# Feed-forward of a hybrid decoder block: the product of gate and up is turned by VectorE and DMAs in place of TensorE

## The chip, the cores and the metric

The kernel runs on one NeuronCore of one Trainium2 chip. That core has TensorE (PE in the profile; PEld is its weight load), VectorE (DVE), ScalarE (ACT), GpSimd (POOL), and SyncE (SP), whose queue starts nearly all transfers here. The metric is the device time of one launch in microseconds, lower is better.

## The reference

One decoder layer over 512 tokens of 1024 features, all in float32. A token mixer (retention and forgetting attention, merged by gates) comes first; it is left alone here but for its last step. What matters is the end:

```python
x = x + merged @ w_out[l]

h2 = rmsnorm(x, g_ffn[l])
ff = (jax.nn.silu(h2 @ w_gate[l]) * (h2 @ w_up[l])) @ w_down[l]
x = x + ff
```

`w_gate` and `w_up` are 1024 x 2816, `w_down` is 2816 x 1024. The norm's factor per token, `rsqrt(mean(x*x) + eps)`, is applied behind the products, as a scale for each token.

## The kernel before

Activations of the residual stream are held with features on the partitions: `x1[p, m, t]` is feature 128 m + p of token t. A float32 product is made of three matmuls: both operands are split into a rounded high part (made by ScalarE, a cast) and a remainder (made by VectorE, a subtraction), and high by high, low by high and high by low are summed in PSUM.

**Gate and up.** The columns of both weights are cut into six groups, `GROUPS = [512] * 5 + [256]`. Each group's pair of products is computed with a Strassen-like scheme of seven block products (`gu`), in the order y (A12), x (A11), S1, S2, S3, S4, A22. Each is 24 matmuls with a 128 x 128 block of the activations as weights and 512 (in the last group 256) weight columns as the moving side. Activations are stationary, so results have tokens on the partitions: four tiles of 128 tokens each. The blocks' sums (`sum_of`, line 947), their casts (line 938) and remainders (line 939) go through a ring of three buffers (`ring_parts`), and each half of a block feeds 12 matmuls.

Three pairs of accumulators are used: `x_`, `z_` (tag `acc`) and `y_` (tag `sc`). `x_` is started by A11, copied to `us` slot 0 by ScalarE (`keep(0, x_)`, line 1033), and then added to by S2, copied again (slot 1), added to by S3, copied (slot 2), and added to by A22. So S2's first matmul writes a bank that `keep(0)` reads. `z_` is copied once (slot 3).

`us[tp]` is a tile of 4 slots of 512 columns for each of the two token pairs. At a group's end slot 0 and slot 2 hold silu(gate) * up for the four token tiles (lines 1087 and 1094); `hs[g]` names these four views. The tiles have the tags `us0` and `us1` in a pool with one buffer for a tag, so the tile of the next group lies in the same memory.

**Turning.** The down product needs the hidden features on the partitions. `put_h(g, cs)` does it in the next group: for each chunk of 128 hidden features, four TensorE transposes (`turn`, line 75) into a `tp` bank, then one ScalarE copy (line 1023) to `pf[:, chunk, :]`. Two chunks go behind the product y, two in the middle of the product x. The last group's two chunks are turned among the first matmuls of the down product.

**The norm.** In group 0 alone, four small matmuls sum the squares, `rsqrt` (12 tiny VectorE instructions) makes `rstd2`, and then the first gate is scaled (lines 1065 and 1066). In the text this lies ahead of the sums for S3.

**Down.** `whole(k, ms)` adds hidden chunk k (8 to 21) to all 8 output banks; `prepare(k)` loads and splits its operands. `p_sums` and the last loop do chunks 0 to 7 with another Strassen-like scheme. There, `raw` (a weight load) and `u2` use the memory of `us0` and `us1`.

**Order.** TensorE's instructions are pinned in the order in which they are written (`pinned`), and VectorE's in the gate and up stage as well (`queue`). ScalarE's and SyncE's order is set by the tile framework's scheduler when the kernel is built. Semaphores, and the wait of a new tile for the old tile in its memory, are the framework's too.

Of the kernel before, what the change touches and what calls it, by code (L numbers as in the profile page):

```python
# [9 lines left out]
F32 = mybir.dt.float32  # L10
F32R = mybir.dt.float32r
# [3 lines left out]
ALU = mybir.AluOpType  # L15
AX = mybir.AxisListType

P = 128
# [35 lines left out]
def block_kernel(ctx: ExitStack, tc, x, xT, c_early, c_tab, c_late, w_qf, w_tok, w_vg, w_a, w_y, w_o, w_gu, w_gl, w_dn, w_dh, out):  # L54
# [19 lines left out]
    def turn(o, src):  # L74
        in_order(nc.tensor.transpose(out=o, in_=src, identity=ident))  # L75

    def f32(ap):
        return ap.bitcast(F32)
# [12 lines left out]
    def bank(tag):  # L91
        return ps.tile([P, 512], F32, name=tag, tag=tag, bufs={"acc": 4, "sc": 2, "tp": 2}[tag])
# [71 lines left out]
    def gffn(k):  # L164
        return ce[:, C_GFFN + k:C_GFFN + k + 1]
# [229 lines left out]
    def queue(ins):  # L395

        after(ins, turn_of[0])
        turn_of[0] = ins
        return ins
# [478 lines left out]
    def split_x(j, at, f):  # L878
        cast = nc.scalar.copy(out=xfh[j][:, at, :], in_=f)
        tt(out=xfl[j][:, at, :], in0=f, in1=f32(xfh[j])[:, at, :], op=ALU.subtract)  # L880
        return cast

    def x_sums(j):

        fx = tmp.tile([P, 7, HT], F32, name="fx", tag="fx")
        for m2 in range(2):
            act(out=fx[:, 2 * m2:2 * m2 + 2, :], in_=x1[:, 2 * j + m2, :].rearrange("p (s t) -> p s t", s=2), func=AF.Copy, scale=gffn(2 * j + m2))
        tt(out=fx[:, S1, :], in0=fx[:, A21, :], in1=fx[:, A22, :], op=ALU.subtract)
        tt(out=fx[:, S2, :], in0=fx[:, S1, :], in1=fx[:, A11, :], op=ALU.subtract)
        tt(out=fx[:, S3, :], in0=fx[:, A11, :], in1=fx[:, A21, :], op=ALU.subtract)  # L890
        tt(out=s4[:, j, :], in0=fx[:, S2, :], in1=fx[:, A12, :], op=ALU.add)
        split_x(j, slice(S1, S3 + 1), fx[:, S1:S3 + 1, :])

    for mp in range(4):
        def evac_o(m2, acc):
            m = 2 * mp + m2
            xn = x1[:, m, :]
            hi, lo = (f[mp][:, 2 * m2:2 * m2 + 2, :].rearrange("p s t -> p (s t)") for f in (xfh, xfl))
            tt(out=xn, in0=acc, in1=xn, op=ALU.add)
            act(out=hi, in_=xn, func=AF.Copy, scale=gffn(m))  # L900
            stt(out=lo, in0=xn, scalar=gffn(m), in1=f32(hi), op0=ALU.mult, op1=ALU.subtract)
            if m == 0:
                act(out=sqs, in_=xn, func=AF.Square)
            else:
                sq2 = tmp.tile([P, S], F32, name="sq2", tag="sq2")
                act(out=sq2, in_=xn, func=AF.Square)
# [43 lines left out]
    def sums_in_parts(g, b, c):  # L950
        return [part(f) for f in [sum_of(g, b, c, v) for v in range(2)]]

    def gu(os, parts, slot, new, w, by_bank=False, middle=None):
        steps = [(j, tp) for j in range(4) for tp in range(2)]
        for i, (j, tp) in enumerate(sorted(steps, key=lambda s: s[1]) if by_bank else steps):
            if i == 4 and middle:
                middle()
# [57 lines left out]
    fp = None  # L1015
    hs = {}

    def put_h(g, cs):
        for c in cs:
            pb = bank("tp")  # L1020
            for t in range(NT):
                turn(pb[:, t * P:(t + 1) * P], hs[g][t][:, c * P:(c + 1) * P])
            nc.scalar.copy(out=pf[:, 4 * g + c, :], in_=pb)

    pinned[0] = True
    for g, w in enumerate(GROUPS):
        us = [fq.tile([P, 4, 512], F32, name=f"us{tp}", tag=f"us{tp}") for tp in range(2)]
        us = [f[:, :, :w] for f in us]
        x_, z_, y_ = [bank("acc") for _ in range(2)], [bank("acc") for _ in range(2)], [bank("sc") for _ in range(2)]

        def keep(slot, os):
            for tp in range(2):
                nc.scalar.copy(out=us[tp][:, slot, :], in_=os[tp][:, :w])  # L1033
# [25 lines left out]
        parts = sums_in_parts(g, B11, B22)  # L1059
        gu(x_, parts, S2, False, w)  # L1060
        keep(1, x_)
        if g == 0:
            turn_of[0] = rsqrt(rstd2, pb[:, 0:NT], 1.0 / D, [P, NT], "n1", behind=turn_of[0])
        for tp in range(2):
            queue(tt(out=us[tp][:, 0, :], in0=y_[tp][:, :w], in1=us[tp][:, 0, :], op=ALU.add))
# [26 lines left out]
        for tp in range(2):  # L1092
            act(out=us[tp][:, 2, :], in_=x_[tp][:, :w], func=AF.Silu, scale=rstd2[:, tp + 2:tp + 3])
            queue(stt(out=us[tp][:, 2, :], in0=us[tp][:, 3, :], scalar=rstd2[:, tp + 2:tp + 3], in1=us[tp][:, 2, :], op0=ALU.mult, op1=ALU.mult))
# [15 lines left out]
            if k == NF - 1:  # L1110
                tt(out=x1[:, m, :], in0=accs[m], in1=x1[:, m, :], op=ALU.add)

    whole(HALF, (0, 1, 4, 5, 2, 3))
    put_h(len(GROUPS) - 1, (0, 1))
    prepare(HALF + 1)
    whole(HALF + 1, (0, 1, 4, 5, 2, 3))
    whole(HALF, (6, 7))
    whole(HALF + 1, (6, 7))
    for k in range(HALF + 2, NF):
        prepare(k)  # L1120
        if (k - HALF) % 3 == 2 and k // 3 - 3 < 4:
            p_sums(k // 3 - 3)
        whole(k, range(NK))

    WT = {"raw": (4, F32, (fq, "us0"), (wq, "b3")), "ah": (3, F32R, (wq, "b1"), (fq, "b2f")), "al": (3, F32R, (fq, "r2"), (wq, "r1")), "t": (4, F32, (wq, "b0")),
          "c0": (4, F32R, (wq, "r0")), "c1": (4, F32R, (wq, "b2"))}
    seen = {}

    def wtile(name):

        n, dt, *places = WT[name]
        i = seen.get(name, 0)
        seen[name] = i + 1
        pool, tag = places[i % len(places)]
        return pool.tile([P, n, 512], dt, name=name, tag=tag)

    def split_to(src, tags):
# [58 lines left out]
    u2 = fq.tile([P, 2, 4, HT], F32, name="u2", tag="us1")  # L1196

    def u_tile():
        turns_u[0] += 1
# [151 lines left out]
```

## Time and profile before

| what | value |
|---|---|
| time, median of 3 runs | 709.59 us (708.0 to 709.94) |
| the profiled execution's own time | 709.5 us |
| its span, first to last instruction | 707.7 us |
| TensorE clock granted | 1.0 throughout |
| TensorE transposes of `us` | 88 |
| ScalarE copies from their banks to `pf` | 22 |
| DMA engines, mean over the span (queue of SP) | 31.9% |

The profile is of one execution; about 1.8 us of its time lie outside the span. The busy share of TensorE says that an instruction was in flight, not that it ran at its peak. The chain of waits is followed back from the last instruction: at each step to what released it, or to the instruction ahead of it on its engine. Idle time that the profile sets in brackets is the time just ahead of an instruction, with what ended it.

### The profile page before, as it was taken

The numbers are of one execution on the slowest core, as the hardware profiler recorded it, in microseconds if no ns is written. First come the engines' busy times: TensorE is split into PE (matmuls) and PEld (weight loads), VectorE is DVE, ScalarE is ACT, GpSimd is POOL, SyncE is SP. The second block draws the span as 40 slices with busy tenths as digits, with TensorE's granted clock in tenths as the row PEclk, the third lists the DMA queues.
The fourth block names the chain that finished last, engine by engine and source line by source line (L and its number), as shares of the span: only waits on it lengthen the run. The fifth ranks groups of instructions, "written<-read, shape, count | busy, mean of one in ns | idle before, by whom it ended". The sixth has DMA issues, their size and how long they took to land. (4 is left out here: it accounts for less than half of the span.)

```text
span 707.7 us, 9510 instructions
## 1 busy us (share of the span) xinstructions
PE 699.0 (99%) x3599; PEld 584.6 (83%) x3599; DVE 521.5 (74%) x845; ACT 375.2 (53%) x570; POOL 72.5 (10%) x90
## 2 busy tenths in 40 slices
PE   8999999999999999999998999999999999999998
PEld 6888988888877768888886888888888898888998
DVE  6798487754788665747978877778797779546794
ACT  6677453233567566326565565665656466334251
POOL 0004941201122110000220000000000000000000
PEclk9999999999999999999999999999999999999999
DMA  8900312223432312239410606042140422321221
GB/s 283 419 16 31 120 60 90 76 86 100 128 107 92 101 61 64 91 114 310 165 60 0 239 1 236 2 144 94 61 149 1 149 94 100 117 108 59 82 91 67
DMA packets 24141, 77.29 MB, mean 109 GB/s; under 512 B 2840, under 2 KB 3480, under 8 KB 23584
## 3 DMA queue, kind: packets, MB, share of 16 engines
q1 hardware_dynamic: 23952, 76.67, 31.9%
q8 instruction: 28, 0.46, 0.2%
q14 instruction: 17, 0.14, 0.1%
q10 hardware_dynamic: 144, 0.02, 0.0%
HBM read 73.52 MB, written 2.11 MB: 107 GB/s over the span
## 5 line engine op out<-in xcount | busy, mean ns | idle before, releaser
L72 PE MATMUL acc<-ps,xfh 128*128 128x512 f32 (+1 forms) x576 | 170.2, 375 | 2.3 <-ACT ps L938 1.6
L72 PEld LDWEIGHTS acc<-ps,xfh 128*128 128x128 f32 x576 | 105.2, 188 | 23.9 <-ACT us L1033 2.3
L939 DVE TENSOR_TENSOR ps<-b,ps 128x1024 fp32r<-128x1024 f32 (+1 forms) x84 | 94.8, 1136 | 40.7 <-ACT ps L938 39.9
L938 ACT CAST ps<-b 128x1024 fp32r<-128x1024 f32 (+1 forms) x84 | 82.2, 981 | 52.7 <-PE acc L72 37.0
L72 PE MATMUL acc<-ps,xfl 128*128 128x512 f32 (+1 forms) x288 | 107.0, 372 | 0.0
L154 ACT CAST wh<-raw 128x1024 fp32r<-128x1024 f32 (+1 forms) x44 | 46.1, 1049 | 84.3 <-PE acc L72 80.2
L155 DVE TENSOR_TENSOR wl<-raw,wh 128x1024 fp32r<-128x1024 f32 (+1 forms) x44 | 57.0, 1297 | 17.3 <-ACT wh L154 17.1
L72 PEld LDWEIGHTS acc<-ps,xfl 128*128 128x128 f32 x288 | 54.3, 189 | 8.7
L72 PE MATMUL acc<-xh,wh 128*128 128x512 f32 x128 | 53.2, 416 | 0.0
L947 DVE TENSOR_TENSOR b<-b,b 128x1024 f32<-128x1024 f32 (+1 forms) x48 | 52.3, 1130 | 0.5 <-DMA b<-in_w_gu_dram 0.5
L72 PE MATMUL acc<-wh,xh 128*128 128x512 f32 (+2 forms) x144 | 50.4, 350 | 0.0
L72 PE MATMUL acc<-xh,wl 128*128 128x512 f32 x128 | 50.1, 392 | 0.0
L72 PE MATMUL acc<-xl,wh 128*128 128x512 f32 x128 | 50.0, 390 | 0.0
L72 PE MATMUL acc<-wh,xl 128*128 128x512 f32 (+2 forms) x144 | 49.4, 343 | 0.0
L72 PE MATMUL acc<-wl,xh 128*128 128x512 f32 (+2 forms) x144 | 49.3, 342 | 0.0
L72 PE MATMUL acc<-hl,ps 128*128 128x512 f32 x168 | 40.4, 389 | 0.0
L72 PEld LDWEIGHTS acc<-hl,ps 128*128 128x128 f32 x168 | 31.5, 188 | 6.6
L1033 ACT COPY us<-acc 128x512 f32<-128x512 f32 (+1 forms) x48 | 26.4, 551 | 18.3 <-PE acc L72 16.6
L977 DVE TENSOR_TENSOR ps<-raw,ps 128x1024 fp32r<-128x1024 f32 x14 | 17.1, 1224 | 21.7 <-ACT ps L974 21.7
L72 PEld LDWEIGHTS acc<-wh,xh 128*128 128x128 f32 x144 | 27.2, 189 | 3.6 <-ACT wh L154 0.2
L72 PEld LDWEIGHTS acc<-wh,xl 128*128 128x128 f32 x144 | 27.1, 189 | 3.2
L72 PEld LDWEIGHTS acc<-wl,xh 128*128 128x128 f32 x144 | 27.2, 189 | 2.9
(297 smaller groups left out, 1501.7 us busy)
## 6 DMA issues: line engine op xcount, KB each, us to landing
b<-in_w_gu_dram SPq DMA_DIRECT2D x40, 512.0 KB, 4.4
raw<-in_w_a_dram SPq DMA_DIRECT2D x16, 512.0 KB, 3.6
raw<-in_w_dn_dram SPq DMA_DIRECT2D x14, 512.0 KB, 4.4
blk<-in_w_vg_dram SPq DMA_DIRECT2D x8, 512.0 KB, 9.9
raw<-in_w_tok_dram SPq DMA_DIRECT2D x8, 512.0 KB, 3.6
raw<-in_w_y_dram SPq DMA_DIRECT2D x8, 512.0 KB, 3.7
raw<-in_w_o_dram SPq DMA_DIRECT2D x8, 512.0 KB, 3.9
raw<-in_w_dh_dram SPq DMA_DIRECT2D x4, 1024.0 KB, 4.9
```

Source lines behind the costliest of these rows:

```text
L72: in_order(nc.tensor.matmul(o, **kw))
L154: split_raw.last = (nc.scalar.copy(out=h[:, :width], in_=raw[:, :width]), tt(out=l[:, :width], in0=raw[:, :width], in1=f32(h)[:, :width], ...
L155: tt(out=l[:, :width], in0=raw[:, :width], in1=f32(h)[:, :width], op=ALU.subtract))
L938: nc.scalar.copy(out=h, in_=raw)
L939: low = tt(out=l, in0=raw, in1=f32(h), op=ALU.subtract)
L947: queue(tt(out=raws[g][b][v], in0=raws[g][b][v], in1=raws[g][c][v], op=ALU.add))
L977: tt(out=l, in0=raw, in1=f32(h), op=ALU.subtract)
L1033: nc.scalar.copy(out=us[tp][:, slot, :], in_=os[tp][:, :w])
```

## The change

`us0` and `us1` become one tile `us` of 8 slots (slots 0 to 3 and 4 to 7 are the old ones). The product is turned in two steps. `turn_h(g, t)` is one VectorE transpose for token tile t: it turns each square of 32 x 32 of the 128 x 512 tile (128 x 256 in the last group) by itself, and writes into the odd slots with a step of 4 elements. `put_h(g)` then moves squares to their partitions: 16 DMAs on SP's queue, each from 32 partitions to 32 partitions of `pf`, with runs of 128 elements (64 KB each, in the last group 32 KB). Token tiles 0 and 1 of a group are turned at the end of the group, tiles 2 and 3 and the 16 DMAs come in the next group, behind the remainder for the second half of its product x; in the last group all come at its end.

So that the pieces lie in natural token order in `pf`, tile t must hold tokens t, t+4, t+8 and so on. `quads` reads the residual stream that way where the operands of gate and up are made: ScalarE's high part, its squares and the copy in `x_sums`, and VectorE's remainder read with a step of 4 elements.

In group 0 the norm's `rsqrt` and the first gate are placed behind the sums for S3; in other groups the gate stays ahead of them.

The down product begins with banks 6 and 7 and runs each chunk whole, since no transposes use the `tp` banks. `raw` and `u2` become parts of one last tile with the tag `us`.

```diff
+    def quads(f):
+        return f.rearrange("p (m t) -> p t m", t=4)
...
-            act(out=hi, in_=xn, func=AF.Copy, scale=gffn(m))
-            stt(out=lo, in0=xn, scalar=gffn(m), in1=f32(hi), op0=ALU.mult, op1=ALU.subtract)
+            act(out=hi, in_=quads(xn), func=AF.Copy, scale=gffn(m))
+            stt(out=lo, in0=quads(xn), scalar=gffn(m), in1=f32(hi), op0=ALU.mult, op1=ALU.subtract)
...
-    def put_h(g, cs):
-        for c in cs:
-            pb = bank("tp")
-            for t in range(NT):
-                turn(pb[:, t * P:(t + 1) * P], hs[g][t][:, c * P:(c + 1) * P])
-            nc.scalar.copy(out=pf[:, 4 * g + c, :], in_=pb)
+    def turn_h(g, t):
+        n = GROUPS[g] // P
+        to = hs[g][:, 1:2 * n:2, :].rearrange("p c (q j t) -> p c q j t", q=4, t=4)[:, :, :, :, t]
+        queue(nc.vector.transpose(out=to, in_=hs[g][:, (0, 4, 2, 6)[t], :n * P].rearrange("p (c q j) -> p c q j", q=4, j=32)))
+
+    def put_h(g):
+        n = GROUPS[g] // P
+        for p in range(4):
+            for q in range(4):
+                nc.sync.dma_start(out=pf[32 * q:32 * q + 32, 4 * g:4 * g + n, p * P:(p + 1) * P], in_=hs[g][32 * p:32 * p + 32, 1:2 * n:2, q * P:(q + 1) * P])
...
-        us = [fq.tile([P, 4, 512], F32, name=f"us{tp}", tag=f"us{tp}") for tp in range(2)]
-        us = [f[:, :, :w] for f in us]
+        hs[g] = fq.tile([P, 8, 512], F32, name="us", tag="us")
+        us = [hs[g][:, 4 * tp:4 * tp + 4, :w] for tp in range(2)]
...
             gu(y_, ahead[g], A12, True, w)
-            put_h(g - 1, (0, 1))
             second = [ahead[g, 1], part(raws[g][B11][1])]
-            gu(x_, second, A11, True, w, middle=lambda: put_h(g - 1, (2, 3)))
+            for t in (2, 3):
+                turn_h(g - 1, t)
+            put_h(g - 1)
+            gu(x_, second, A11, True, w)
             keep(0, x_)
...
+        if g:
+            gate_0()
+        parts = sums_in_parts(g, B12, B22)
         if g == 0:
             turn_of[0] = rsqrt(rstd2, pb[:, 0:NT], 1.0 / D, [P, NT], "n1", behind=turn_of[0])
-        for tp in range(2):
-            queue(tt(out=us[tp][:, 0, :], in0=y_[tp][:, :w], in1=us[tp][:, 0, :], op=ALU.add))
-            act(out=us[tp][:, 0, :], in_=us[tp][:, 0, :], func=AF.Silu, scale=rstd2[:, tp:tp + 1])
-        parts = sums_in_parts(g, B12, B22)
+            gate_0()
...
-        hs[g] = [us[0][:, 0, :], us[1][:, 0, :], us[0][:, 2, :], us[1][:, 2, :]]
+        for t in range(2):
+            turn_h(g, t)
+        if g == len(GROUPS) - 1:
+            for t in (2, 3):
+                turn_h(g, t)
+            put_h(g)
...
-    whole(HALF, (0, 1, 4, 5, 2, 3))
-    put_h(len(GROUPS) - 1, (0, 1))
-    prepare(HALF + 1)
-    whole(HALF + 1, (0, 1, 4, 5, 2, 3))
-    whole(HALF, (6, 7))
-    whole(HALF + 1, (6, 7))
-    for k in range(HALF + 2, NF):
-        prepare(k)
+    for k in range(HALF, NF):
+        if k > HALF:
+            prepare(k)
         if (k - HALF) % 3 == 2 and k // 3 - 3 < 4:
             p_sums(k // 3 - 3)
-        whole(k, range(NK))
+        whole(k, (6, 7, 0, 1, 4, 5, 2, 3) if k == HALF else range(NK))
```

More of the change, by code (lines that the diff above doesn't have):

```diff
@@ L897, in evac_o @@
             xn = x1[:, m, :]
[L898 removed]
+            hi, lo = (f[mp][:, 2 * m2:2 * m2 + 2, :].rearrange("p s (b m) -> p (s b) m", b=2) for f in (xfh, xfl))
             tt(out=xn, in0=acc, in1=xn, op=ALU.add)
[L900 to L901 removed]
+            act(out=hi, in_=quads(xn), func=AF.Copy, scale=gffn(m))
+            stt(out=lo, in0=quads(xn), scalar=gffn(m), in1=f32(hi), op0=ALU.mult, op1=ALU.subtract)
             if m == 0:
[L903 removed]
+                act(out=sqs.rearrange("p (t m) -> p t m", t=4), in_=quads(xn), func=AF.Square)
             else:
                 sq2 = tmp.tile([P, S], F32, name="sq2", tag="sq2")
[L906 removed]
+                act(out=sq2.rearrange("p (t m) -> p t m", t=4), in_=quads(xn), func=AF.Square)
                 gp.tensor_tensor(out=sqs, in0=sqs, in1=sq2, op=ALU.add)
@@ L951, in sums_in_parts, with gu @@
         return [part(f) for f in [sum_of(g, b, c, v) for v in range(2)]]
-    def gu(os, parts, slot, new, w, by_bank=False, middle=None):
+    def gu(os, parts, slot, new, w, by_bank=False):
         steps = [(j, tp) for j in range(4) for tp in range(2)]
-        for i, (j, tp) in enumerate(sorted(steps, key=lambda s: s[1]) if by_bank else steps):
-            if i == 4 and middle:
-                middle()
+        for j, tp in sorted(steps, key=lambda s: s[1]) if by_bank else steps:
             h, l = parts[j // 2]
@@ L1061, in block_kernel, with gate_0 @@
         keep(1, x_)
+        def gate_0():
+            for tp in range(2):
+                queue(tt(out=us[tp][:, 0, :], in0=y_[tp][:, :w], in1=us[tp][:, 0, :], op=ALU.add))
+                act(out=us[tp][:, 0, :], in_=us[tp][:, 0, :], func=AF.Silu, scale=rstd2[:, tp:tp + 1])
+        if g:
+            gate_0()
+        parts = sums_in_parts(g, B12, B22)
         if g == 0:
             turn_of[0] = rsqrt(rstd2, pb[:, 0:NT], 1.0 / D, [P, NT], "n1", behind=turn_of[0])
-        for tp in range(2):
-            queue(tt(out=us[tp][:, 0, :], in0=y_[tp][:, :w], in1=us[tp][:, 0, :], op=ALU.add))
-            act(out=us[tp][:, 0, :], in_=us[tp][:, 0, :], func=AF.Silu, scale=rstd2[:, tp:tp + 1])
-        parts = sums_in_parts(g, B12, B22)
+            gate_0()
         if g + 1 < len(GROUPS):
```

9 lines of the change are left out of this document (6 added, 3 removed).

## The prediction

> **What bounds the kernel now.** I read the page first, then the chain of waits in the gate and up stage, then the timelines of single engines inside one group, and last who releases SP's loads. The page's span and busy times:
>
> ```profile
> span 707.7 us, 9510 instructions
> PE 699.0 (99%) x3599; PEld 584.6 (83%) x3599; DVE 521.5 (74%) x845; ACT 375.2 (53%) x570; POOL 72.5 (10%) x90
> ```
>
> TensorE is the bound, so work taken off it counts in full, as long as nothing makes it wait. The chain of waits (start, length, what) shows one group, 443.5 to 483.8, and the turn in the down product:
>
> ```profile
> 443.54 5.44 PE sc L72 x24
> 448.99 0.87 PE tp L75 x8
> 449.86 2.75 PE acc L72 x12
> 452.60 0.87 PE tp L75 x8
> 453.48 30.30 PE acc L72 x132
> ...
> 590.89 0.87 PE tp L75 x8
> ```
>
> Nothing but TensorE is on it: a product of 24 matmuls lasts 5.44 us, eight transposes 0.87 us, two such blocks in a group. One group more shows, in the table by stretches (length, then PE, PEld, DVE, ACT, POOL busy), how much the others have left; the first row is the output projection:
>
> ```profile
> 327.00:361.00 34.00, 34.00 (x152) 28.16 (x151) 27.70 (x37) 18.47 (x28) 7.11 (x5) 1.00 0.51 185
> 443.30:483.60 40.30, 40.30 (x186) 33.11 (x185) 32.33 (x33) 23.70 (x31) 0.00 (x0) 1.00 0.30 104
> ```
>
> **What goes.** From the groups by line:
>
> ```profile
> L75 PE MATMUL tp<-ctab,us x88: 270/272/273, 408.6 to 591.5; 128*128 128x128 f32 x88
> L1023 ACT COPY pf<-tp x22: 580/587/596, 409.3 to 591.8; 128x512 f32<-128x512 f32 x22
> ```
>
> 88 transposes are 11 blocks of 0.87 = 9.6 us of TensorE: two blocks in each of groups 1 to 5 (1.74 a group), one in the down product. The 22 copies (22 x 0.587 = 12.9 us) are on ScalarE, which has 16 us of 40 free in a group, so they are worth nothing by themselves.
>
> **The norm in group 0.** TensorE's and VectorE's timelines there:
>
> ```profile
> 383.93 0.39 PE L72 MATMUL acc<-ps,xfh 128*128 128x512 f32 x1
> 385.94 0.50 PE L72 MATMUL acc<-ps,xfh 128*128 128x512 f32 x1 [1.62 <-ACT ps L938]
> 386.28 0.40 PE L72 MATMUL acc<-ps,xfl 128*128 128x512 f32 x1
> 387.20 0.73 PE L72 MATMUL acc<-ps,xfh 128*128 128x512 f32 x2 [0.53 <-DVE ps L939]
> ...
> 378.76 0.16 DVE L115 TENSOR_SCALAR n1v<-tp 128x4 f32<-128x4 f32 x1 [0.72 <-PE tp L72]
> ...
> 381.03 1.28 DVE L1065 TENSOR_TENSOR us<-sc,us 128x512 f32<-128x512 f32 x2
> 382.23 2.35 DVE L947 TENSOR_TENSOR b<-b,b 128x1024 f32<-128x1024 f32 x2
> ```
>
> Matmuls follow each other every 0.227 us (5.44 / 24). The gap from 383.93 to 385.94 loses 1.78, that to 387.20 0.69, two short ones between and behind 0.11 each: 2.7 us. VectorE did the norm and the first gate (378.76 to 382.23) ahead of the sums that S3 needs. With the sums first they end 3.5 us earlier, 381.1, casts and remainders by about 383.5, and S3 finds them: **2.7 us** gained. What is late next is the first remainder for S4, behind the norm and gate: S3's remainders to 383.5, norm and gate 3.5, a silu 0.6, a cast 1.05 and the remainder 1.23 end near 389.9, against a need at 390.0 (S3's start at 384.2, one product, two matmuls), so I cost it at nothing; up to 0.5 us if wrong.
>
> **What comes: the turns.** VectorE's timeline at the turn of a group:
>
> ```profile
> 441.61 1.40 DVE L1087 SCALAR_TENSOR_TENSOR us<-us,rstd 128x512 f32<-128x512 f32 x2
> ...
> 446.29 0.75 DVE L1094 SCALAR_TENSOR_TENSOR us<-us,rstd 128x512 f32<-128x512 f32 x1
> 447.38 1.23 DVE L939 TENSOR_TENSOR ps<-b,ps 128x1024 fp32r<-128x1024 f32 x1 [0.35 <-ACT ps L938]
> 448.53 2.35 DVE L947 TENSOR_TENSOR b<-b,b 128x1024 f32<-128x1024 f32 x2
> ...
> 330.76 1.41 DVE L901 SCALAR_TENSOR_TENSOR xfl<-x,ce,xfh 128x512 fp32r<-128x512 f32 x2
> ...
> 342.29 2.46 DVE L901 SCALAR_TENSOR_TENSOR xfl<-x,ce,xfh 128x512 fp32r<-128x512 f32 x2
> ```
>
> The trace has no VectorE transpose. Of the rows with 512 elements, the cheapest step is 0.60 (381.03 to 382.23 above is two), the usual 0.70 (1.40 for two), the dearest 1.23 (2.46 for two). I take 0.70, the row of the same plain kind, and keep 0.60 and 1.23. In "VectorE: DVE Perf Modes", section "The three transpose paths", the Trainium skill gives 311 ns for 128 elements of two bytes; an estimate by that, with 384 more elements at the 1.07 ns by which the steps of 1.15 (1024 elements, 447.38 to 448.53) and 0.60 differ, is 0.72, and no run here shows it. The last gate product ends at 447.04; two turns: 448.44; the pinned remainder (a step of 1.15): 449.59; two turns: **450.99**. S1's sums (2.35) and first remainder (1.23) then end near 454.6; S1 starts at 454.3 (S2's start below, less a product and 1.74) and reads it with its third matmul, so this by itself costs about nothing.
>
> **What comes: the wait.** A new tile in old memory waits for all that used the old one, not only for the part that it overwrites. The evidence is SP: the two halves of B22 are read by the remainders at 468.72 and 471.31, and both halves are loaded anew only when the second ends (VectorE, then SP):
>
> ```profile
> 468.72 1.23 DVE L939 TENSOR_TENSOR ps<-b,ps 128x1024 fp32r<-128x1024 f32 x1 [1.49 <-ACT ps L938]
> 471.31 1.23 DVE L939 TENSOR_TENSOR ps<-b,ps 128x1024 fp32r<-128x1024 f32 x1 [1.36 <-ACT ps L938]
> ...
> 472.56 0.80 SPq L927 DMA_DIRECT2D b<-in_w_gu_dram  x2
> ```
>
> `us` is one tile with one buffer. So `keep(0, x_)`, its first writer in a group, must wait for all 16 DMAs of the group before, and S2 must not write `x_` until `keep(0)` has read it. When do the 16 land? SP's issues in a run at the start of the kernel, the one SBUF-to-SBUF group (ns, min/median/max) with its time to landing, and the landing of the output's DMAs:
>
> ```profile
> 8.29 0.43 SPq L192 DMA_DIRECT2D spare<-in_w_tok_dram  x1
> 8.77 0.43 SPq L188 DMA_DIRECT2D xf<-in_xT_dram  x1
> 9.24 0.43 SPq L192 DMA_DIRECT2D spare<-in_w_tok_dram  x1
> ...
> L660 SPq DMA_DIRECT2D tk<-tk x8: 462/467/531, 180.9 to 236.0; - x8
> ...
> DMA to landing us min/median/max: 2.2/3.9/4.5
> ...
> DMA to landing us min/median/max: 1.7/2.0/2.5
> ```
>
> In a run an issue takes a step of 0.47. The SBUF-to-SBUF ones take 0.467 alone, where a single load takes 0.33, so up to 0.61 in a run. I take the middle, 0.54. Landing: 2.1 (between 1.7 and 3.9). The last of 16 is issued at 450.99 + 0.05 + 15 x 0.54 = 459.1 and lands at 461.2. ScalarE and TensorE around that point:
>
> ```profile
> 455.59 1.27 ACT L1033 COPY us<-acc 128x512 f32<-128x512 f32 x2 [0.89 <-PE acc L72]
> 456.76 1.05 ACT L938 CAST ps<-b 128x1024 fp32r<-128x1024 f32 x1
> ...
> 461.29 0.62 PE L72 MATMUL acc<-ps,xfh 128*128 128x512 f32 x2
> ```
>
> The second of the last two matmuls, 461.52, is S2's first. Without transposes it could run at 459.8; the copy (0.62) must end before it. With the wait it runs at 461.2 + 0.05 + 0.62 = **461.9**. So the wait eats the 1.74 and 0.4 more: +0.4 in each of groups 1 to 4, **+1.6**. Behind the copies on ScalarE stand that of `z_` (now 461.04) and the first silu, and VectorE's first gate sum waits for them; S3's operands, which come behind it, have 5.4 us more. S2's casts stand there too, if the scheduler put the copies ahead of them (a rival, below). No weight load is due on SP until 467, so its 16 issues delay nothing else.
>
> In group 5 products are half as long, but the turned group is a full one:
>
> ```profile
> 565.62 0.74 DVE L1094 SCALAR_TENSOR_TENSOR us<-us,rstd 128x512 f32<-128x512 f32 x1
> 566.39 0.69 DVE L939 TENSOR_TENSOR ps<-b,ps 128x512 fp32r<-128x512 f32 x1
> ...
> 574.34 0.40 PE L72 MATMUL acc<-ps,xfh 128*128 128x256 f32 x2
> ```
>
> Gate product to 566.36, turns to 567.76, remainder (0.62) 568.38, turns 569.78, last issue 577.9, landed 580.0, copy (0.37) 580.45. S2's first matmul is the second of the row at 574.34, 574.47 now: **+6.0**.
>
> **The rest.** The block at 590.89 and a gap of 0.24 at the start of the down product go: -1.1. Group 5's turns and 16 DMAs come before chunks 20 and 21 are needed, over 60 us later. Reads with a step of 4 (24 on ScalarE, 8 on VectorE) I cost at nothing: the output projection has 15.5 us of ScalarE and 6.3 of VectorE free in 34. At the dearest rate above the 8 on VectorE add 8 x 0.53 = 4.2, still inside; only the last pair stands right before group 0, up to 1.5 us.
>
> **Sum**, against the profiled execution's 709.5 (span 707.7 and 1.8 around it; the median is 709.59): -2.7 + 1.6 + 6.0 - 1.1 = +3.8, **713.3 us**. Its own range: a step of 0.47 gives 708, 0.61 718; a landing of 3.9 adds 9, 1.7 takes 2, a turn of 0.60 takes 2. I set 706 to 722.
>
> **Rivals.**
>
> *Hidden transfer, not slower.* If the wait doesn't hold `keep(0)` (only the parts overwritten count, or the puts land before 459.1 in full groups and well before 573 in the last), all transposes are a gain: 709.5 - 2.7 - 9.6 - 0.3 = 696.9. It decides from a step of about 0.40 on, in full groups. For it: TensorE is 99% busy and VectorE has 8 us free in a group. Against: the loads of B22, and 16 issues at 0.47 alone are 7.5 us.
>
> *Slow turns.* At 1.23 four turns end 2.1 us later, and so do the DMAs: 5 x 2.1 = +10.6, 724. For it: the turns write, and `quads` reads, with a step of 16 bytes, which no row here shows; the row at 342.29 shows that this shape can take 1.23. Against: that row is slow beside GpSimd, which is idle in the groups. The Trainium skill speaks for this rival: in "SBUF — State Buffer", section "Door 1: The DMA port swizzle (why `[64,N]` ≈ `[32,N]`)", it says that SBUF works in lines of 16 bytes, that two accesses in a line are needed for full rate, and that each access to a new line pays. No run here shows it yet.
>
> *Blocked casts.* If ScalarE's order has `keep(0)` ahead of S2's first cast, that cast comes after both copies: the landing + 1.27 + 1.05, and its remainder 1.2 later, some 2.4 us more than above in a full group and 1.3 in the last: +10.9, 724. For it: ScalarE now does `keep(0)` at 455.59 and that cast at 456.76. Against: the cast would be ready by about 455.6, before the DMAs land, and order on ScalarE follows readiness where the text has it otherwise (S2's casts stand ahead of the copies at 461.04).
>
> Slow turns and blocked casts together: 735.
>
> **Chances.** Forecast 0.36, hidden transfer 0.20, slow turns 0.18, blocked casts 0.18, both 0.08. The range 696 to 727 leaves out the last case and the edges. A measurement of this kernel tells about 0.3% (2.1 us) from no change: faster (below 707.5) 0.22, from the hidden transfer and the low end of the forecast; within 0.12; slower 0.66.
>
> **What would show it.** Right: no L75 rows on `us`; in each group TensorE idle once, ahead of S2, about 2 us (6 in the last), released by ScalarE's copy L1033, which itself waits for the DMAs to `pf`; no gap at 384 to 387. Wrong: turns far from 0.70; S1, not S2, late; L1033 at its old place behind A11; DMA issues on SP at another step than 0.54.

## The result, and the profile after

| | time, median (lowest to highest) | ratio to before |
|---|---|---|
| before | 708.9 us (708.0 to 709.94), 4 runs | |
| after | 741.68 us (740.65 to 743.1), 4 runs | 1.0463 [1.0437, 1.049] |

The change costs 33 us. The forecast was 713.3 us with a range of 696 to 727: the sign was right, the size was not, and the range did not reach. The profiled execution took 741.01 us. From its page, span, busy times, granted clock in 40 slices, and the head of the chain that ended last:

```profile
span 739.3 us, 9446 instructions
PE 701.1 (95%) x3511; PEld 580.2 (78%) x3511; DVE 540.3 (73%) x869; ACT 374.2 (51%) x548; POOL 71.7 (10%) x90
...
PEclk9999999999999999999999999899999979999999
...
PE 72%; DVE 8%; SPq 6%; ACT 5%; DMA 4%; issue 3%; POOL 0%; ACTq 0%; DVEq 0%; POOLq 0%
```

TensorE issues 88 matmuls fewer (3511 after 3599) and is nevertheless busy for longer in a span that is 31.6 us longer: it now has idle time, and some of its work went at a lower clock. SP's queue, which was on no chain before, has 6% of it. The new chain stands in the chain of waits of one group (start, length, what):

```profile
407.14 0.68 DVE us L1109
...
408.78 1.05 DVE us L1024
409.84 1.05 DVE ps L943
410.89 1.90 DVE us L1024 x2
...
412.85 0.72 SPq L1031
...
422.00 0.60 SPq L1031
...
422.65 2.00 DMA pf<-us
...
424.75 0.59 ACT us L1041
...
425.38 0.80 PE acc L72
```

Read it from the top: the last gate product (L1109), two turns (L1024), a remainder, two turns, 16 issues on SP in a row (L1031), the last landing, ScalarE's copy of `x_` (L1041, `keep(0)`), S2's first matmul. Each waits for the one above. TensorE's timeline shows what that does to S2, in a full group and in the last:

```profile
421.21 0.39 PE L72 MATMUL acc<-ps,xfh 128*128 128x512 f32 x1
425.38 0.80 PE L72 MATMUL acc<-ps,xfh 128*128 128x512 f32 x1 [3.79 <-ACT us L1041]
425.98 0.63 PE L72 MATMUL acc<-ps,xfl 128*128 128x512 f32 x1
...
428.82 0.62 PE L72 MATMUL acc<-ps,xfh 128*128 128x512 f32 x2
...
597.13 0.28 PE L72 MATMUL acc<-ps,xfh 128*128 128x256 f32 x1
604.72 0.58 PE L72 MATMUL acc<-ps,xfh 128*128 128x256 f32 x1 [7.31 <-ACT us L1041]
```

One matmul to the next should take 0.227 us. From 421.21 to 425.38 that loses 3.95, and 7.47 in the last group. Behind the gap, from its second matmul on, a matmul is followed by the next only after 0.43 us (six times there), until 428.54. The table by stretches (length, then PE, PEld, DVE, ACT and POOL busy, then the granted clock) names the reason; the last two rows are the same place in the next group:

```profile
418.00:421.00 3.00, 3.00 (x15) 2.46 (x14) 2.94 (x4) 2.11 (x2) 0.00 (x0) 1.00 0.41 106
425.00:428.00 3.00, 2.62 (x6) 2.14 (x7) 2.64 (x4) 3.00 (x7) 0.00 (x0) 0.54 0.00 0
...
471.00:474.00 3.00, 2.51 (x6) 2.03 (x7) 2.53 (x4) 3.00 (x6) 0.00 (x0) 0.50 0.00 0
474.00:477.00 3.00, 3.00 (x9) 2.32 (x9) 2.25 (x2) 1.19 (x3) 0.00 (x0) 0.60 0.00 0
```

After the idle time the clock is about half. Adding up the steps that stand out, from the first matmul of group 0 to the end of the kernel, by what each has above 0.227 us (0.12 for 256 columns):

| where TensorE loses time (us) | before | after |
|---|---|---|
| ahead of S2, groups 1 to 5 | 0 | 3.95, 5.09, 3.77, 3.74, 7.47: 24.0 |
| steps at half clock behind these waits | 0 | 8.1 |
| ahead of and in S1 | 0 | 2.4, 0.7, 0.7, 0.7, 2.7: 7.2 |
| start of group 0 | 0.3 | 3.8 |
| group 0, ahead of S3 | 2.7 | 0.3 |
| 88 transposes | 9.6 | 0 |

The differences come to 24.0 + 8.1 + 7.2 + 3.5 - 2.4 - 9.6 = 30.8 us. From the first matmul of group 0 to the end of the span it is 33.9 us (346.5 before, 380.4 after); the other 3.1 are smaller steps, half of them the step behind S2's first matmul. The spans differ by 31.6 alone since the profiled execution after began group 0 at 358.84, that before at 361.16. Why, the table can't say.

### The profile page after: what moved, and what is told of

The parts are those of the page before. It is cut to its first block, busy times and chain, and to the rows that moved or that the text cites. A ratio compares the mean times of both kernels' runs of the same rounds, so it can differ in the third digit from the quotient of the medians.

```text
span 739.3 us, 9446 instructions
## 1 busy us (share of the span) xinstructions
PE 701.1 (95%) x3511; PEld 580.2 (78%) x3511; DVE 540.3 (73%) x869; ACT 374.2 (51%) x548; POOL 71.7 (10%) x90
## 4 chain that ended last, share of the span: by engine, by line
PE 72%; DVE 8%; SPq 6%; ACT 5%; DMA 4%; issue 3%; POOL 0%; ACTq 0%; DVEq 0%; POOLq 0%
PE acc L72 54%; PE sc L72 12%; SPq L1031 6%; PE tp L72 5%; DVE us L1024 2%; DVE ps L943 2%; PE tp L75 2%; DMA b<-in_w_gu_dram 2%; DMA pf<-us 1%; ACT ps L942 1%; ACT xfh L904 1%; DVE us L1109 1%; ACT sq L910 1%; ACT fx L891 1%; DMA cb<-cd 0%
## 5 line engine op out<-in xcount | busy, mean ns | idle before, releaser
L72 PE MATMUL acc<-ps,xfh 128*128 128x512 f32 (+1 forms) x576 | 179.0, 390 | 29.5 <-ACT us L1041 23.2
L72 PEld LDWEIGHTS acc<-ps,xfh 128*128 128x128 f32 x576 | 110.1, 198 | 58.1 <-ACT us L1041 28.1
L72 PE MATMUL acc<-ps,xfl 128*128 128x512 f32 (+1 forms) x288 | 110.9, 385 | 1.0 <-DVE xfl L905 1.0
L72 PEld LDWEIGHTS acc<-ps,xfl 128*128 128x128 f32 x288 | 57.0, 198 | 10.6 <-DVE xfl L905 1.3
L1041 ACT COPY us<-acc 128x512 f32<-128x512 f32 (+1 forms) x48 | 25.0, 556 | 36.3 <-DMA pf<-us 23.7
L72 PE MATMUL sc<-ps,xfh 128*128 128x512 f32 (+1 forms) x96 | 28.9, 374 | 1.6 <-DVE ps L943 0.9
```

The lines of the kernel that those rows point to most:

```text
L72: in_order(nc.tensor.matmul(o, **kw))
```

## The experiments

The theory after the result: the wait forecast is there, S2 behind the landing of all 16 DMAs; it is longer since a turn takes 1.06 us and a step from issue to issue 0.65, idle time brings half clock, and reads with a step delay group 0. Rivals for single parts stand in the expectations. Line numbers shift by a few between kernels; every operation keeps its name.

| run | time (us) | ratio to before |
|---|---|---|
| e1, before with the norm later | 705.43 | 0.9952 [0.9939, 0.9964] |
| e2, two tiles for the slots | 722.2 | 1.0196 [1.0175, 1.0216] |
| e3, plain order of tokens | 738.83 | 1.0418 [1.0402, 1.0434] |
| e4, TensorE kept busy in the wait | 735.04 | 1.0365 [1.0343, 1.0387] |
| e5, turns write densely | 733.95 | 1.0339 [1.0302, 1.0377] |
| e6, two queues (SP, GpSimd) | 714.31 | 1.0073 [1.0052, 1.0095] |
| e7, two queues (SP, ScalarE) | 740.12 | 1.0443 [1.0412, 1.0475] |
| e8, e2 and e6 together | 714.19 | 1.0071 [1.0045, 1.0097] |
| e9, tokens in pairs | 729.79 | 1.0292 [1.0265, 1.032] |
| e10, e8 with tokens in pairs | 707.77 | 0.9983 [0.997, 0.9997] |
| e11, e10 with later turns | 717.93 | 1.0131 [1.0103, 1.016] |
| e12, e10 with ScalarE's copies in order | 701.46 | 0.99 [0.9881, 0.9919] |

**e1: the moved norm alone**, put into the kernel before.

```diff
-        if g == 0:
-            turn_of[0] = rsqrt(rstd2, pb[:, 0:NT], 1.0 / D, [P, NT], "n1", behind=turn_of[0])
-        for tp in range(2):
...
+        if g:
+            gate_0()
         parts = sums_in_parts(g, B12, B22)
+        if g == 0:
+            turn_of[0] = rsqrt(rstd2, pb[:, 0:NT], 1.0 / D, [P, NT], "n1", behind=turn_of[0])
+            gate_0()
```

> The kernel before with one edit: in group 0 the norm and the first gate stand behind the sums for S3. Theory (TensorE's gap at 384 to 387 came from VectorE doing the norm first): 2.7 us less than before, ratio 0.996, and no gap over 0.2 us ahead of S3 in group 0. Rival (the late remainder for S4 takes its place): within 0.5 us of before.

705.43 against 709.2 for the kernel before beside it: 3.8 us by the medians (2.6 to 4.3 by the interval). The gap is gone. TensorE's timeline at the start of S3, which is the second matmul of the middle row:

```profile
381.88 0.39 PE L72 MATMUL acc<-ps,xfl 128*128 128x512 f32 x1
382.11 0.89 PE L72 MATMUL acc<-ps,xfh 128*128 128x512 f32 x2
382.83 0.40 PE L72 MATMUL acc<-ps,xfl 128*128 128x512 f32 x1
```

The steps there lose 0.16 and 0.11, where the kernel before lost 2.7. S4 loses nothing. So the trace accounts for some 2.4 us; the profiled execution was 1.8 us ahead already at the start of group 0, in a part that the edit doesn't touch, and where that comes from stays open. This part of the change is a gain, and alone it is 0.5% faster than the kernel before.

**e2: the wait of a new tile for the old one.** The odd slots, which the turns write and the DMAs read, get a tile of their own; `Slots` takes slot i from tile i % 2.

```diff
-        hs[g] = fq.tile([P, 8, 512], F32, name="us", tag="us")
-        us = [hs[g][:, 4 * tp:4 * tp + 4, :w] for tp in range(2)]
+        hs[g] = [fq.tile([P, 4, 512], F32, name=n, tag=n) for n in ("ua", "ub")]
+        us = [Slots(hs[g], tp, w) for tp in range(2)]
```

> The changed kernel, but the even slots of `us` (gate products, first copy) and the odd slots (turned squares, later copies) are two tiles, so the first copy of x no longer waits for the 16 transfers; the transfers themselves are the same. Theory (the wait of the new tile for the transfers out of the old one costs 16.6 us ahead of S2 in groups 1 to 4, and the half clock behind it 7.3 more): about 24 us less in these groups, 0.6 a group given back at S3, where the second copy now waits; in group 5 the wait moves to S3 and falls from 7.5 to about 5. Total 716 to 720. Rival (VectorE's longer work and the transfers themselves hold TensorE up, not the tile's reuse): 736 or more.

722.2 us, 2 above the expected span. The waits of S2 are gone: `keep(0)` writes slot 0, and its tile has no DMA as a user. In their place S3 waits, 2.80, 1.34, 1.35, 1.36 and 5.62 us, for the copies into the odd slots (TensorE's timeline, group 2):

```profile
469.11 0.39 PE L72 MATMUL acc<-ps,xfh 128*128 128x512 f32 x1
470.68 0.50 PE L72 MATMUL acc<-ps,xfh 128*128 128x512 f32 x1 [1.18 <-ACT ub L1048]
```

So a wait belongs to the tile, not to the part of it that is overwritten, as the prediction took it. Splitting the tile moved the wait by one product and took 19.5 us. What is left ahead of S3 isn't the landing in this group: the last DMA is issued at 465.5 and has landed by 467.5, while the copies start at 469.08 behind two casts on ScalarE. e12 comes back to that.

**e3: the reads of every fourth token.** `quads` reads in a row, everything else as in the changed kernel.

```diff
-        return f.rearrange("p (m t) -> p t m", t=4)
+        return f.rearrange("p (t m) -> p t m", t=4)
```

> The changed kernel, but the token tiles hold 128 tokens in a row (reads with a step of 1), so the turned squares land in the wrong token order; all else is the same. Theory (reads with a step of 16 bytes slow ScalarE and VectorE in the output projection, and group 0 starts late): the 3.8 us that TensorE loses at 362 to 372 fall to 0.3, ScalarE's 128x512 activations from 1.1 to 0.7 us, total 738. Rival (order on VectorE, not the reads): 741 or more.

738.83 us: the reads cost 2.9 us. One row by source each, after and then e3 (duration in ns, min/median/max):

```profile
L904 ACT ACTIVATE xfh<-x,ce x8: 1192/1206/1234, 327.2 to 364.4; 128x512 fp32r<-128x512 f32 x8
```

```profile
L904 ACT ACTIVATE xfh<-x,ce x8: 707/713/724, 327.8 to 361.8; 128x512 fp32r<-128x512 f32 x8
```

And TensorE's timeline of the changed kernel at the start of group 0, where it waits for them:

```profile
363.52 0.50 PE L72 MATMUL acc<-ps,xfh 128*128 128x512 f32 x1 [0.44 <-ACT xfh L904]
365.02 0.50 PE L72 MATMUL acc<-ps,xfl 128*128 128x512 f32 x1 [1.00 <-DVE xfl L905]
...
371.48 0.73 PE L72 MATMUL sc<-ps,xfh 128*128 128x512 f32 x2 [0.94 <-DVE ps L943]
```

The 3.8 us lost at the start of group 0 fall to 0.3 in e3. Most of the 24 slow reads on ScalarE are hidden by the output projection; those for the last pair of blocks are not.

**e4: is it the idle time that brings the half clock?** TensorE runs small products into an unused bank ahead of S2.

```diff
+        if g:
+            spare_bank = bank("tp")
+            for i in range(16 if w == 512 else 30):
+                mm(spare_bank, lhsT=xfh[0][:, A11, 0:P], rhs=xfh[1][:, 0:2, :], start=True, stop=True)
         gu(x_, parts, S2, False, w)
```

> The changed kernel with 16 matmuls more (30 in the last group) into an unused bank ahead of S2 in groups 1 to 5, so that TensorE is busy for 3.6 us (6.8) of its wait. Theory (the matmuls behind the wait run at a step of 0.43 instead of 0.23 us because TensorE was idle before): with the idle time down to 1.5 us or less the steps of 0.43 go, 9.5 us in all, and nothing is lost by the added work: 730 to 734. Rival (the slower clock has another cause, or work added costs time): 741 or more.

735.04 us, 6.6 less by adding work, 1 above what was expected. In the table by stretches, the place behind the wait:

```profile
424.00:427.00 3.00, 2.83 (x13) 2.01 (x12) 1.89 (x3) 2.51 (x5) 0.00 (x0) 1.00 0.00 1
```

Clock 1.00, and of the steps at half rate behind S2's waits (some 50 in the changed kernel) none is left. From the last gate product to S2's first matmul it is as long as before (17.58 us for 17.57 in the group shown), with work in between that nobody needs, so what is gained is the clock's part alone.

**e5: the price of a turn.** Turns of the five full groups write single elements in a row.

```diff
+        if n == 4:
+            to = hs[g][:, 1 + 2 * t, :].rearrange("p (c q j) -> p c q j", q=4, j=32)
```

> The changed kernel, but the turns of the five full groups write in a row of single elements instead of a step of 4 (the last group's turns as before; the pieces then land in the wrong places of pf, so the down product's input is wrong in value, not in amount). Theory that the 1.06 us of a turn come from writing with a step of 16 bytes: the turns fall to about 0.7 us (step 0.6), the fourth ends about 1.4 us earlier, so do the 16 DMAs, and S2's idle time falls from about 3.9 to 2.5 us in four groups, that of the last from 7.5 to 6.0, with less half clock: about 741.7 - 5 x 1.4 - 3 = 732 us. Rival, that a VectorE transpose of this size costs 1.06 us whatever its step: turns stay at 1.06 us, 741.7 us within 2.

733.95 us, near the 732 of the theory of the write step. The row of the turns, after and then e5:

```profile
L1024 DVE STREAM_TRANSPOSE us<-us x24: 610/1058/1123, 407.8 to 622.6; 128x512 f32<-128x512 f32 x20, 128x256 f32<-128x256 f32 x4
```

```profile
L1026 DVE STREAM_TRANSPOSE us<-us x24: 622/674/709, 409.9 to 615.5; 128x512 f32<-128x512 f32 x20, 128x256 f32<-128x256 f32 x4
```

A turn is 0.67 us by itself, near the 0.70 that the prediction took from a plain row; the step of 16 bytes adds 0.38. (The four small turns of the last group still write with the step.) The gain doesn't show where it was expected: S2 still loses 3.91, 4.39, 3.30, 3.32 and 7.38 us, not 2.5 and 6.0. It is S1's loss that goes, from 7.2 to 1.2, so TensorE comes to S2 earlier and waits there nearly as long. From the last gate product to S2's first matmul the five groups take 16.15, 17.05, 15.95, 15.97 and 15.21 us, where the changed kernel takes 17.57, 18.72, 17.39, 17.37 and 16.80: 7.5 less in all, about the 7.7 us gained.

**e6, e7, e8: the issues.** Every second DMA goes through another queue: GpSimd's (e6), ScalarE's (e7), GpSimd's with the two tiles of e2 (e8).

```diff
-                nc.sync.dma_start(out=pf[32 * q:32 * q + 32, 4 * g:4 * g + n, p * P:(p + 1) * P], in_=hs[g][32 * p:32 * p + 32, 1:2 * n:2, q * P:(q + 1) * P])
+                (nc.sync if q % 2 else nc.gpsimd).dma_start(out=pf[32 * q:32 * q + 32, 4 * g:4 * g + n, p * P:(p + 1) * P], in_=hs[g][32 * p:32 * p + 32, 1:2 * n:2, q * P:(q + 1) * P])
```

> The changed kernel, but every second of the 16 DMAs of a group is started from GpSimd's queue, the others from SP's. Theory that 16 issues in a row at 0.645 us each set the end of the wait: 8 issues are over 5.2 us earlier, the last lands about when S2 is due, S2's idle time falls from about 4 us to below 0.5 in four groups and from 7.5 to about 2.3 in the last, and the half clock behind it goes: 741.7 - 16 - 5 - 8 = about 712 us. Rival, that the transfers themselves or the landing set it, or that GpSimd's issue takes over 1 us: the time stays above 730 us.

> The same with ScalarE's queue for every second DMA. The theory of the issue step gives the same 712 us, if ScalarE's share of the issues does not hold up its casts; it has about 16 us of 40 free in a group, and 8 issues of 0.6 us are 4.8. Rival: the issues stand in order ahead of S1's casts and wait there for the turns, S1 and S2 become late on ScalarE instead, and the time is 720 to 735 us.

> The changed kernel with the odd slots in a tile of their own and every second DMA on GpSimd's queue. Two tiles alone left waits of S3 of 2.80, 1.35 three times and 5.62 us. The theory says that both waits are the last landing: these go but for about 0.5 us in the last group, 722.2 - 12 = about 710 us, near the time before (709), since S1's waits (about 7 us in all) and those at the start of group 0 (3.5 us) stay. Rival, that GpSimd's issues are slow or that contention takes the gain: 715 to 722 us.

e6 gives 714.31 us, 2 above the expectation: S2 loses 0.82 us in group 2, 1.80 in the last and nothing in the others, in place of 24.0 in all (S3 loses 0.3 in groups 1, 3 and 4). The rows by source of the issues and of their time to landing, after and then e6:

```profile
L1031 SPq DMA_DIRECT2D pf<-us x96: 586/599/1615, 412.8 to 633.3; - x96
...
DMA to landing us min/median/max: 1.8/2.0/3.6
```

```profile
L1031 SPq DMA_DIRECT2D pf<-us x48: 594/600/1221, 413.9 to 600.5; - x48
L1031 POOL DMA_DIRECT2D pf<-us x48: 533/548/745, 414.7 to 599.3; - x48
...
DMA to landing us min/median/max: 1.8/2.7/4.7
```

An issue takes its engine as long as before; with two engines at it the landing is 0.7 us later at the median, and still 27 of the 33 us are gone. So the row of 16 issues was the largest piece of the wait.

e7 gives 740.12 us, worse than its rival said. ScalarE works in order, and its timeline shows what stood behind the eight issues:

```profile
453.96 1.06 ACT L942 CAST ps<-b 128x1024 fp32r<-128x1024 f32 x1 [1.04 <-PE sc L72]
459.72 5.48 ACTq L1031 DMA_DIRECT2D pf<-us  x8
465.31 2.00 ACT L942 CAST ps<-b 128x1024 fp32r<-128x1024 f32 x2 [10.29 <-DMA pf<-us]
```

The issues wait for the turns (the last ends at 459.69) until 459.72, and the casts for S1 come behind them at 465.31; TensorE then waits at S1, 4.5 to 5.4 us in a full group. The name in the bracket, a DMA to `pf`, is the profile's guess: the cast reads nothing of `pf`, and it starts 0.1 us after the last issue ends. A queue is only worth what stands behind it.

e8 gives 714.19, no better than e6 and 4 above the expectation: the waits of S3 fall from 2.80, 1.35 (three times) and 5.62 to 0.67, 0.37 (three times) and 1.83, which is 8.9 and not 12, and S1's and group 0's losses remain.

**e9: any step, or 16 bytes?** Another order of tokens that still gives runs for the DMAs: a tile holds every second token of one half, so reads and the turns' writes have a step of 8 bytes. A DMA moves twice as many runs of half the length.

```diff
-        return f.rearrange("p (m t) -> p t m", t=4)
+        return f.rearrange("p (m u) -> p u m", u=2)
...
-        to = hs[g][:, 1:2 * n:2, :].rearrange("p c (q j t) -> p c q j t", q=4, t=4)[:, :, :, :, t]
+        to = hs[g][:, 1::2, :n * P].rearrange("p q (c h j u) -> p c q h j u", h=2, j=32, u=2)[:, :, :, t % 2, :, t // 2]
...
-                nc.sync.dma_start(out=pf[32 * q:32 * q + 32, 4 * g:4 * g + n, p * P:(p + 1) * P], in_=hs[g][32 * p:32 * p + 32, 1:2 * n:2, q * P:(q + 1) * P])
+                nc.sync.dma_start(out=pf[32 * q:32 * q + 32, 4 * g:4 * g + n, :].rearrange("i c (h b e) -> i b (c h) e", h=2, b=4)[:, p], in_=hs[g][32 * p:32 * p + 32, 1 + 2 * q, :n * P].rearrange("i (c e) -> i c e", e=64))
```

> The changed kernel with another order of tokens that is right as well: a tile holds every second token of one half, so reads of the residual stream and the turns' writes have a step of 2 elements (8 bytes) in place of 4, and a DMA to pf moves runs of 64 elements (256 bytes), 8 a partition instead of 4. Theory that it is the line of 16 bytes that costs (two accesses in a line for full rate): ScalarE's reads fall to 0.71 us, the turns to 0.7, and the time to that of plain reads and dense turns together, 741.7 - 2.9 - 7.7 = about 731 us, if DMAs of twice as many runs cost the same. Rival, that any step costs in proportion: reads 0.95, turns 0.88, about 736 us. Rival, that runs of 256 bytes slow the issue or the landing: a step of over 0.8 us for an issue would give 741.7 or more.

729.79 us, near the 731 of the theory. The rows by source of e9:

```profile
L904 ACT ACTIVATE xfh<-x,ce x8: 741/758/768, 328.0 to 362.0; 128x512 fp32r<-128x512 f32 x8
...
L1024 DVE STREAM_TRANSPOSE us<-us x24: 407/673/716, 404.8 to 610.6; 128x512 f32<-128x512 f32 x20, 128x256 f32<-128x256 f32 x4
...
L1031 SPq DMA_DIRECT2D pf<-us x96: 586/608/1699, 408.5 to 621.8; - x96
```

Per read on ScalarE: 0.713 us in a row, 0.758 with a step of 8 bytes, 1.206 with 16. Per turn: 0.674, 0.673, 1.058. It isn't the step as such, nor does it grow in proportion to the step. Runs of 256 bytes cost the issue 0.01 us.

**e10, e11, e12: what is left.** e10 joins pairs of tokens, two tiles and two queues. e11 also puts the turns and DMAs behind the sums for S1:

```diff
-            for t in (2, 3):
-                turn_h(g - 1, t)
-            put_h(g - 1)
             gu(x_, second, A11, True, w)
-            keep(0, x_)
             parts = sums_in_parts(g, B11, B12)
+            for t in (2, 3):
+                turn_h(g - 1, t)
+            put_h(g - 1)
+            keep(0, x_)
```

e12 is e10 with an order for ScalarE's copies in groups 1 to 5 (`after(a, b)` puts a behind b on their engine; `kept[slot]` is a slot's last copy, `part.cast` the last cast made). In groups 1 to 4 the copies of `z_` stand ahead of the first silu and of S3's casts; S2's copies stand behind S3's casts and ahead of S4's:

```diff
+                if 0 < g < len(GROUPS) - 1:
+                    after(silu, kept[3])
...
+            if b == B12 and 0 < g < len(GROUPS) - 1:
+                after(part.cast, kept[3])
...
+            keep(1, x_, part.cast)
+            if g + 1 == len(GROUPS):
+                keep(3, z_)
...
+        parts = [part(raws[g][B22][0])]
+        if g:
+            after(part.cast, kept[1])
```

> The same order of tokens with the odd slots in a tile of their own and every second DMA on GpSimd's queue. From the 714.2 us of the run without the new order: the 2.9 at the start of group 0 go, the turns end 1.4 us earlier, which takes most of the 0.7 of S1 in four groups: 714.2 - 2.9 - 2.5 = about 709 us. Rival, that DMAs of 8 runs a partition cost the gain: 712 to 716.

> The same with the turns of token tiles 2 and 3 and the DMAs behind the sums for S1 on VectorE. The theory says that S1 is late only because VectorE turns ahead of its sums: S1's idle time goes (0.7 in each group, 1.7 more in group 1, 2.6 in the last), and the last DMAs land by about 464 in a full group, ahead of S3: about 704 us, below the 705.4 of the moved norm alone. Rival: in the short last group the turns then hold up S2's sums or S3 waits for the DMAs: 707 to 710.

> The run with pairs of tokens, two tiles and two queues (707.8 us), with ScalarE's order set by hand in groups 1 to 5: the copies of z_ into the odd slots stand ahead of the first silu and of S3's casts, those of S2's result right behind S3's casts and ahead of S4's. There, S3's first matmul was released by these copies, which stood on ScalarE at 463.61, behind S3's casts, although the last DMA can have landed at about 457.6 (issues to 454.99 and 2.6 to land): idle 2.80, 1.07, 1.07, 1.07 and 1.84 us. Theory: it is the order on ScalarE that is late, not the transfer, and these go but for about 1 us in the last group: 707.8 - 6.8 = about 701 us. Rival: the transfers do land late, the copies then hold up the silu and S3's casts behind them, and the time is 708 to 712 us.

e10 gives 707.77 us, as expected: level with the kernel before. e11 is a miss, 717.93 where 704 was expected. S1's losses do go (none is left in groups 1 to 4), but S3 now waits 2.8 to 3.1 us in full groups and 3.9 in the last, although the DMAs land before it, as meant: in group 2 the last is issued at 459.74 and lands some 2 us later, while the four copies stand at 465.49 on ScalarE, behind a cast for S4. So in full groups the rival that S3 waits for the DMAs has the place right and not the cause. e12 takes the matter up from e10. ScalarE's timeline in e10 and in e12, the same group, then TensorE's in e10:

```profile
461.52 2.19 ACT L942 CAST ps<-b 128x1024 fp32r<-128x1024 f32 x2 [0.46 <-DVE b L951]
463.61 2.04 ACT L1048 COPY ub<-acc 128x512 f32<-128x512 f32 x4
```

```profile
454.44 1.27 ACT L1054 COPY ub<-acc 128x512 f32<-128x512 f32 x2 [0.41 <-PE acc L72]
455.92 1.34 ACT L1092 ACTIVATE ua<-ua,rstd 128x512 f32<-128x512 f32 x2 [0.21 <-DVE ua L1091]
457.70 2.21 ACT L942 CAST ps<-b 128x1024 fp32r<-128x1024 f32 x2 [0.45 <-DVE b L951]
459.88 1.26 ACT L1054 COPY ub<-acc 128x512 f32<-128x512 f32 x2
```

```profile
463.92 0.39 PE L72 MATMUL acc<-ps,xfh 128*128 128x512 f32 x1
465.22 0.50 PE L72 MATMUL acc<-ps,xfh 128*128 128x512 f32 x1 [0.91 <-ACT ub L1048]
```

In e10 the two copies of `z_` and the two of S2's result stand together, behind S3's casts; S3's first matmul waits for the third of them. In e12 the copies of `z_` run at 454.44, released by TensorE and not by a DMA: the pieces had landed. S3's wait is gone in groups 2 to 4 (0.67 in group 1, 1.40 in the last), and the time is 701.46 us, as the theory has it: what remained at S3 in groups 1 to 4 of e10 was an order on ScalarE that was fixed when the kernel was built. In the last group the copies follow the landing. e12 beats both kernels, and e1 too (their intervals do not meet). Whether the later turns of e11 gain anything under such an order was not tried.

## Why the prediction was wrong

**Right.** The chain of steps was named as it is: the turns, a remainder, the turns, 16 issues on SP, the landing, `keep(0)`, S2. The evidence from the loads of B22 (a tile is waited for as a whole) held: e2 moved the wait with the tile. The rival of the hidden transfer (696.9) is refuted. The 88 transposes went, and with them 9.6 us; the block in the down product too. The norm gained about what was said (2.7 forecast, 2.4 in the table above). S2's casts were not caught behind the copies, as ScalarE's timeline of the changed kernel shows, so the rival of blocked casts is refuted:

```profile
418.63 2.19 ACT L942 CAST ps<-b 128x1024 fp32r<-128x1024 f32 x2 [2.51 <-DVE b L951]
424.75 2.05 ACT L1041 COPY us<-acc 128x512 f32<-128x512 f32 x4 [3.92 <-DMA pf<-us]
```

**Mis-sized: the issue step.** Taken as 0.54 us, between 0.47 and 0.61, from eight SBUF-to-SBUF issues of 0.467. Here an issue takes 0.599 and a step 0.653 (412.85 to 422.65 in 15 steps), outside the bounds. In a full group that is 15 x 0.113 = 1.7 us; as there are five, about 8.5 in all. The upper bound had been put together from a single row of another shape and the step of a run of loads.

**Mis-sized: the turn.** Taken as 0.70, measured 1.06 (two in a row 1.90 to 1.99). From the gate product's end to the end of the fourth turn, 3.95 us became 4.97 (407.82 to 412.79): 1.0 a group, about 5 in all; against turns of 0.67, as in e5, it is 7.5. This is two thirds of the way to the rival of slow turns (1.23). The Trainium skill, in "SBUF — State Buffer", section "Door 1: The DMA port swizzle (why `[64,N]` ≈ `[32,N]`)", had the rule, lines of 16 bytes of which two accesses are needed for full rate; e9 agrees with it, 0.673 us with two elements in a line and 1.058 with one. The prediction gave that rule a chance of 0.18 and 0.08 where both rivals met; the row it leaned on had neither a step nor a transpose.

These two and the landing (2.00 for 2.1) account for one group: from the last gate product to S2's first matmul the prediction had 14.9 us (447.04 to 461.9), the trace 17.6 (407.82 to 425.38); 1.0 for the turns, 1.7 for the issues and 0.1 less for the landing are 2.6 of the 2.7. In the last group the prediction had 14.1 and the trace 16.8, the same 2.7. Two things come on top. In group 2 one issue took 1.6 us. In group 1 the last gate product ends 5.34 us behind the group's first matmul, in groups 2 to 4 3.66, so the chain starts 1.7 late; in the kernel before it is 3.66 there too, with the norm alone moved (e1) 4.96. Moving the norm costs nothing by itself, but part of it comes back as soon as a chain hangs on the end of group 0.

**Left out: the clock.** The prediction counted an idle time ahead of S2 of about 2 us, and no price for what comes after it. The waits of 3.7 to 5.1 and 7.5 us each brought 6 to 21 matmuls at half rate: 8.1 us. The length of a single wait doesn't decide it: of two waits of 3.59 us in e9 that in group 3 brought no slow step and that in group 4 eight, and one of 1.88 in the last group of e6 brought eleven. In e8 even the start of group 0, where no wait is over 1.3 us, was followed by eight steps of 0.43; in the changed kernel the same waits were not. The table by stretches of e8, the waits and then the stretch behind them:

```profile
369.80:373.20 3.40, 1.84 (x7) 0.94 (x6) 2.84 (x5) 3.40 (x6) 0.72 (x1) 1.00 0.00 0
373.30:376.60 3.30, 3.30 (x9) 2.59 (x8) 3.16 (x5) 1.78 (x3) 0.00 (x0) 0.50 0.00 0
```

So the forecast's own waits of 2 us were at risk as well as that of 6. The Trainium skill, in "TensorE: Matmul & The Clock Gate", section "🔬 Part 1: The HAM clock gate (the "warmup" mystery)", says that an idle window of about 3.4 us halves the clock. The traces agree only in part: every wait of 3.7 us and more brought half clock, and so did these shorter ones.

**Taken as nothing: S1 and the reads.** The turns were said to let S1 through "by itself costs about nothing"; turns at 1.06 pushed its sums back, and S1 lost 0.7 in groups 2 to 4 and more in groups 1 and 5, 7.2 us in all. With turns at 0.67 the 0.7 is gone in groups 2 to 4 of e5, e9, e10 and e12. In the changed kernel this is no cost beside the wait, but a piece of it: S2 starts when the chain ends, whether S1 was late or not (e5). The reads of every fourth token were costed at nothing, up to 1.5: they took 2.9 (e3).

So the forecast failed at one step, the sum of the wait: its path was right, and its two durations were read from rows of another kind. Of the 28 us that it is short, 15 are that wait (31.2 us in S1 and ahead of S2, where its own sum has 1.74 and 0.4 in each of four groups and 1.74 and 6.0 in the last), 8.1 the clock and 3.5 the start of group 0. The range failed as it let these be wrong one at a time: the high issue step (718) and the slow turns (724) together, without the clock, would have been about 729.

## What to carry to other kernels

When work is taken off the bounding engine and given to a chain of others, lay that chain end to end against the slack of one stage, and ask of each duration whether its row has the same access pattern; a chain that overruns costs the overrun in every round, and on TensorE the clock besides. A buffer that DMAs still read should be a tile of its own, the DMAs should be shared among queues behind which nothing urgent stands, and tokens are best interleaved by two (8 bytes) and not by four. Where a wait seems to be a DMA's, look first at where the waiting instruction stands on its own engine: from e10 to e12 that order alone was worth about 6 us.

## What the hardware showed that was not expected

- With four-byte elements, a step of 8 bytes costs a read on ScalarE 6% (0.713 to 0.758 us for 512) and a VectorE transpose's write nothing; a step of 16 bytes costs them 69% and 57% (1.206 and 1.058).
- Half clock lasted 6 to 10 matmuls of 512 columns behind an idle time of 3.7 to 5.1 us, 2.6 to 4.3 us by the step of 0.43. Useless matmuls in the wait removed it. The length of a single wait didn't decide: one of 3.59 us brought it in group 4 of e9 and not in group 3, and in e8 four of 0.6 to 1.3 us in a row did.
- An issue of a DMA from 32 partitions to 32 takes SP 0.60 us and GpSimd 0.55 with four runs of 512 bytes a partition, 0.61 and 0.58 with eight of 256. From two queues at once the landing is later, 2.7 us for 2.0 at the median.
